# Latent attention with keys in partitions: maxima from a one-pass product, weights summed by additions

## The chip, the cores and the metric

The kernel runs on one core of one Trainium2 chip. The metric is the device time of one execution in microseconds (us). The engines are TensorE (PE, matrix products), VectorE (DVE), ScalarE (ACT), GpSimd (POOL) and SyncE (SP, which issues most of the transfers). The kernel keeps PE's results in eight PSUM banks of 128 partitions by 512 float32 columns, and everything else in SBUF.

## What is computed

The reference is a diffusion transformer of two layers on 256 context tokens and 1024 latent tokens of width 1024. Each layer has an input projection into three groups of heads (gated linear attention, retention, and eight heads of latent attention), an output projection, and a gated convolutional feed-forward part. The change concerns latent attention alone:

```python
def _mla_attend(qn, qr, kn, kr, v):
    s = (jnp.einsum('bqhd,bkhd->bhqk', qn, kn)
         + jnp.einsum('bqhr,bkr->bhqk', qr, kr)).astype(jnp.float32) * MLA_SCALE
    p = jax.nn.softmax(s, axis=-1).astype(v.dtype)
    return jnp.einsum('bhqk,bkhe->bqhe', p, v)
```

A query has 64 features without and 32 with rotation, 96 in all; a head's values have 64. Latent queries see all 1280 keys, context queries the 256 context keys. In the second layer no context output is needed. Everything is float32; a projection or score is computed as three products of the operands' high and low parts (hi by hi, lo by hi, hi by lo).

## The kernel before

A layer is a row of stages: the input projection (`proj`, whose matmuls are those of line 323), then linear attention (`lin`) and latent attention (`mla`) side by side, then the output projection (`wout`) and the feed-forward part. `lin` and `mla` are Python generators, and `weave` takes 1.1 steps of `lin` (`LIN_RATE`) for every step of `mla`. Each step emits some instructions; a scheduler then sets the final order of each engine, which the engine keeps to.

`mla` goes through the eight heads. `prod_v` makes the values of a pair of heads, `prod_qr` the rotated queries of four heads, and `prod_kq` keys and queries of one head, split into hi and lo, in tiles `h` of 96 used partitions (features) by 1280 tokens. What the next head needs is emitted beside the present one (`side`).

A unit is 128 queries of one head; a latent unit does this:

- `scores` (line 919): queries in partitions, keys along the columns, three products each for 512, 512 and 256 keys into three banks (`three` flips between banks 0 to 2 and 3 to 5). DVE takes the maximum of the first 1024 columns (921) and of the last 256 (924) and makes the negated, scaled maximum of both (928). ACT takes the exponentials in two pieces into the tile `w` (932), with their sums as a second output.
- `turn`: PE transposes the ten 128x128 blocks of weights (945) into the unit's own score banks; ACT (949, twice) and DVE (947) copy them to SBUF.
- `values`, once for two units: the value tile of 64 columns is stationary, the turned weights of 128 queries stream through it (969); the first unit writes the upper, the second the lower half of the partitions of bank `av`, in turn. DVE adds the two partial sums (962) and takes the reciprocal of 128x1 (963), POOL makes a diagonal matrix of it (965), PE spreads it by a product with ones (974), ACT copies that (976), and DVE multiplies (979) into a tile `y` for two heads.
- A transfer (983) writes `y` to DRAM (`S.m`) in two pieces per pair of heads; `wout` reads it back.

Layer 0 has two more units per head, the context's queries with 256 keys (`qp == 0`). The rotating buffers that matter are seven of `w2` (weights and turned weights) and five of `dgt`.

Of linear attention, DVE work with both operands in SBUF (lines 693, 703) and POOL products of 128x512 (716) recur below. The splits of weights and activations into hi and lo end in the subtraction of line 213.

Of the kernel before, what the change touches and what calls it, by code (L numbers as in the profile page):

```python
# [9 lines left out]
F32 = mybir.dt.float32  # L10
# [9 lines left out]
T = 1280  # L20
# [54 lines left out]
class Net:  # L75
# [53 lines left out]
    def dgt(self):  # L129
        return self.sb.tile([128, 128], F32, tag="dgt", bufs=5, name=self.nm("dg"))  # L130
# [34 lines left out]
    def wplan(self):  # L165
        """The split weights in the order of their use."""
# [57 lines left out]
    def explog(self, after=None):  # L224
        """The table set with both exp and ln, before a run of them."""
# [22 lines left out]
    def ada(self, l, sets, alloc=None):  # L248
        """Modulation, for both kinds of tokens, of 1024 features at a time: of a section, or of a half of sections 0 and 1."""
# [39 lines left out]
    def modulate(self, l, sec, c0, c1, src, F):  # L289
        """F[k] = src(k) * (1 + scale) + shift; src(k) may be F[k] itself."""  # L290
# [25 lines left out]
    def dense(self, ps, segs, wu, h, ks=range(8)):  # L316
        """ps[:, i, :n] = w.T @ h[:, o:o + n] over 8 K tiles, or the ks of them, for the i-th (o, n) of segs."""
# [8 lines left out]
    def rstd(self, ps, segs, scale, eps, al):  # L326
        """(sum * scale + eps) ** -0.5 in SBUF."""
# [30 lines left out]
    def begin(self, h, n):  # L358
        """The first half of K for the first n tiles of the projection: steps for their weights, then for a K tile of one."""
# [11 lines left out]
    def proj(self, l, b, h, S):  # L371
        """A step for every tile of the projection's columns."""
# [40 lines left out]
        def t3():  # L413
# [11 lines left out]
            # sums of log gates within chunks, [0] from the right and [1] from the left  # L425
# [115 lines left out]
    def lin_tables(self, l, S):  # L541
# [10 lines left out]
        # rows of iota: t + 1, 127 - t, 128 - t, t;  lg: 0..1 by partition (fwd, bwd), 2 + 4 * dir + head  # L552
# [18 lines left out]
    def lin_states(self, l, S):  # L571
        """The chunks' k^T v sums, and from them the state before every chunk, in both directions."""
# [4 lines left out]
        for g in range(5):  # L577
# [4 lines left out]
            for r in range(2):  # L582
# [27 lines left out]
                # the sums lie where the state after their chunk belongs  # L610
# [18 lines left out]
    def lin_chunk_out(self, S, r, c, qv, cs, v, rhs, oS):  # L629
        """o (pair, chunk) = states' part + rhs(h)'s part, into oS."""  # L630
# [44 lines left out]
    def gla_out(self, l, S, g):  # L675
# [11 lines left out]
        def factors(ns):  # L687
            """[0]: q's factor exp(sum from the middle of its block of 2n), [1]: k times its factor."""
# [19 lines left out]
        def expands(i, ns):  # L708
            """q of every head in rows of its own, times its factor."""
# [46 lines left out]
        # products of neighbours and of equal tokens: their sums over a head are columns  # L756
# [69 lines left out]
    def mla(self, l, S):  # L826
        nc, a = self.nc, self.a
# [9 lines left out]
        flip = [0]  # L837

        def three(keep=False):
            b = flip[0] ^ 3  # L840
            if not keep:
                flip[0] = b
            return self.ps[:, b:b + 3, :].rearrange("p a b -> p (a b)")

        def prod_v(p):
            V[p] = [self.hid([128, 5, 128]) for _ in range(2)]
            ps = three(keep=True)
# [7 lines left out]
        def prod_qr(x):  # L855
            QR[x] = [self.yk(F32R), self.yk(F32R)]
            ps, raw = three(keep=True), QR[x][1]
# [18 lines left out]
        def prod_kq(h):  # L876
# [14 lines left out]
            ps = three(keep=True)  # L891
# [15 lines left out]
        def scores(h, qp, i):  # L907
            """Weights of 128 queries, without their sums' division."""
            ctxq = qp == 0
            K, q = Kt[h % 2], Q[h]  # L910
            qs = slice(256 * qp + 128 * i, 256 * qp + 128 * i + 128)
            order = ((0, 0), (1, 0), (0, 1))
            st = self.sm([128, 8])
            sc = three()
            nk = CTX if ctxq else T
            for o in range(0, nk, 512):
                n = min(512, nk - o)
                for x, (qa, ka) in enumerate(order):
                    nc.tensor.matmul(sc[:, o:o + n], q[qa][0:96, qs], K[ka][0:96, o:o + n], start=(x == 0), stop=(x == 2))  # L919
                if o == 512:  # L920
                    nc.vector.tensor_reduce(st[:, 1:2], sc[:, 0:1024], axis=AX.X, op=ALU.max)  # L921
                if o + n < nk:
                    yield
            nc.vector.tensor_reduce(st[:, 0:1], sc[:, o:nk], axis=AX.X, op=ALU.max)
            if ctxq:
                nc.vector.tensor_scalar(st[:, 2:3], st[:, 0:1], -MSCALE, None, op0=ALU.mult)
            else:
                nc.vector.tensor_scalar(st[:, 2:3], st[:, 0:1], st[:, 1:2], -MSCALE, op0=ALU.max, op1=ALU.mult)  # L928
            P = self.w2([128, T], F32)
            # two pieces, for the first bank's transposes to start beside the second  # L930
            for j, (c0, c1) in enumerate([(0, nk)] if ctxq else [(0, 512), (512, nk)]):
                nc.scalar.activation(P[:, c0:c1], sc[:, c0:c1], AF.Exp, bias=st[:, 2:3], scale=MSCALE, accum_out=st[:, 3 + j:4 + j])  # L932
            ready.append(((h, qp, i), P, st, nk // 128, sc))
            yield

        ready, pts, vals, cur = [], [], [], []

        def turn(u):
            (h, qp, i), P, st, nk, sc = u
            pT = self.w2([128, 10, 128], F32)  # L940
            for gi, t0 in enumerate(range(0, nk, 4)):
                n = min(4, nk - t0)
                ps = sc[:, 128 * t0:128 * (t0 + n)].rearrange("p (a b) -> p a b", b=128)
                for t_ in range(n):
                    nc.tensor.transpose(ps[:, t_], P[:, 128 * (t0 + t_):128 * (t0 + t_) + 128], self.ident[:])  # L945
                if gi == 1:
                    nc.vector.tensor_copy(pT[:, t0:t0 + n], ps[:, 0:n])  # L947
                else:
                    nc.scalar.copy(pT[:, t0:t0 + n], ps[:, 0:n])  # L949
                if t0 + n < nk:  # L950
                    yield
            pts.append((pT, st))
            if i:
                vals.append(values(h, qp, [p for p, _ in pts], [t for _, t in pts], nk))
                pts.clear()

        def values(h, qp, pts, sts, nk):
            r = 64 * (h % 2)
            dgs = []
            for st in sts:  # L960
# [507 lines left out]
```

## Time and profile before

| | us |
|---|---|
| median of three runs | 3470.79 (3468.51 to 3471.84) |
| span of the profiled execution | 3473.9 |
| PE busy | 3383.5 (97%) |
| DVE busy | 2227.2 (64%) |
| ACT busy | 1548.3 (45%) |
| POOL busy | 398.5 (11%) |

The profiled execution's own time is that span, 3473.9 us; nothing of it lies around the span in what was recorded. Shares of the whole span are means over stages with different limits, so the table of stretches is to be read by stage. Matmuls are pipelined: the duration of one (some 0.29 to 0.64 us) is longer than the step from one start to the next, so the price of PE's work is read from the starts of a timeline. A float32 matmul that is not split into hi and lo has two records per instruction, a product of hi and lo parts and a transpose have one.

### The profile page before, as it was taken

The numbers are of one execution on the slowest core, as the hardware profiler recorded it, in microseconds if no ns is written. First come the engines' busy times: TensorE is split into PE (matmuls) and PEld (weight loads), VectorE is DVE, ScalarE is ACT, GpSimd is POOL, SyncE is SP. The second block draws the span as 40 slices with busy tenths as digits, with TensorE's granted clock in tenths as the row PEclk, the third lists the DMA queues.
The fourth block names the chain that finished last, engine by engine and source line by source line (L and its number), as shares of the span: only waits on it lengthen the run. The fifth ranks groups of instructions, "written<-read, shape, count | busy, mean of one in ns | idle before, by whom it ended". The sixth has DMA issues, their size and how long they took to land. (4 is left out here: it accounts for less than half of the span.)

```text
span 3473.9 us, 58101 instructions
## 1 busy us (share of the span) xinstructions
PE 3383.5 (97%) x23454; PEld 2919.4 (84%) x23454; DVE 2227.2 (64%) x3787; ACT 1548.3 (45%) x2867; POOL 398.5 (11%) x627
## 2 busy tenths in 40 slices
PE   8999999989999999999999999999999999999998
PEld 6997666768999999899999898766777888888897
DVE  3435878776774444675557734788877765687555
ACT  3334555544453333343334444555563544345433
POOL 0000333331010000000000000333310000001001
PEclk9999999989999999999999999999999999999999
DMA  8654111124223333432223444111124333323331
GB/s 291 203 185 135 29 55 41 40 83 141 74 73 116 122 116 132 147 104 78 75 73 120 161 135 136 36 42 51 38 96 131 96 92 97 97 91 116 98 92 49
DMA packets 174990, 354.95 MB, mean 102 GB/s; under 512 B 15552, under 2 KB 92160, under 8 KB 174720
## 3 DMA queue, kind: packets, MB, share of 16 engines
q1 hardware_dynamic: 174720, 351.23, 31.7%
q8 instruction: 184, 3.01, 0.4%
q14 instruction: 86, 0.70, 0.1%
HBM read 310.01 MB, written 36.44 MB: 100 GB/s over the span
## 5 line engine op out<-in xcount | busy, mean ns | idle before, releaser
L323 PE MATMUL ps<-h,w 128*128 128x320 f32 (+5 forms) x9600 | 1667.4, 334 | 15.1 <-ACT h L212 6.3
L323 PEld LDWEIGHTS ps<-h,w 128*128 128x128 f32 x9600 | 1532.0, 190 | 145.7 <-issue 7.0
L213 DVE TENSOR_TENSOR w<-ws,w 128x1024 fp32r<-128x1024 f32 x360 | 440.1, 1223 | 590.5 <-PE ps L323 294.5
L1180 PE MATMUL ps<-hid,w 128*128 128x256 f32 (+4 forms) x3696 | 576.6, 316 | 1.5 <-ACT hid L212 1.5
L1180 PEld LDWEIGHTS ps<-hid,w 128*128 128x128 f32 x3696 | 538.9, 189 | 36.1 <-issue 7.6
L212 ACT CAST w<-ws 128x1024 fp32r<-128x1024 f32 x360 | 378.8, 1053 | 416.6 <-PE ps L1180 291.2
L919 PE MATMUL ps<-h,h 96*128 96x512 f32 (+1 forms) x1200 | 325.4, 392 | 18.7 <-DVE w L947 14.4
L919 PEld LDWEIGHTS ps<-h,h 96*128 96x128 f32 x1200 | 200.0, 194 | 78.1 <-issue 21.1
L1147 DVE SCALAR_TENSOR_TENSOR t<-u,vec,t 128x642 f32<-128x642 f32 (+3 forms) x176 | 144.6, 821 | 181.9 <-ACT t L1146 181.8
L932 ACT ACTIVATE w<-ps,sm 128x768 f32<-128x768 f32 (+2 forms) x272 | 208.9, 774 | 113.0 <-DVE sm L928 91.2
L1141 ACT COPY u<-ps 128x512 f32<-128x512 f32 (+4 forms) x264 | 118.2, 483 | 310.7 <-PE ps L323 310.7
L1185 DVE SCALAR_TENSOR_TENSOR y<-ps,mod,y 128x320 f32<-128x320 f32 (+5 forms) x376 | 197.0, 557 | 69.0 <-PE ps L1180 68.3
L945 PE MATMUL ps<-ident,w 128*128 128x128 f32 x1312 | 222.3, 287 | 12.1 <-ACT w L932 12.0
L945 PEld LDWEIGHTS ps<-ident,w 128*128 128x128 f32 x1312 | 152.0, 144 | 70.6 <-issue 35.5
L965 POOL TENSOR_SCALAR dg<-ident,sm 128x128 f32<-128x128 f32 x144 | 99.8, 697 | 954.7 <-DVE sm L963 833.4
L1137 POOL MEMSET u<- 128x1 f32 (+1 forms) x264 | 20.9, 102 | 1616.9 <-DVE t L1148 1462.4
L969 PE MATMUL ps<-w,hid 128*64 128x128 f32 x2624 | 196.8, 282 | 3.8 <-DVE y L979 2.0
L969 PEld LDWEIGHTS ps<-w,hid 128*64 128x64 f32 x2624 | 151.8, 139 | 41.2 <-issue 29.1
L921 DVE TENSOR_REDUCE sm<-ps 128x1 f32<-128x1024 f32 x128 | 156.3, 1221 | 43.8 <-PE ps L919 38.8
L949 ACT COPY w<-ps 128x256 f32<-128x256 f32 (+1 forms) x272 | 128.2, 474 | 94.0 <-PE ps L945 92.0
L716 POOL TENSOR_TENSOR hid<-hid,hid 128x512 f32<-128x512 f32 x108 | 146.3, 1371 | 98.5 <-ACT hid L696 69.0
L1146 ACT ACTIVATE t<-u,vec 128x642 f32<-128x642 f32 (+3 forms) x176 | 153.8, 874 | 0.4
(195 smaller groups left out, 3279.4 us busy)
## 6 DMA issues: line engine op xcount, KB each, us to landing
ws<-in_up_dram SPq DMA_DIRECT2D x176, 512.0 KB, 3.6
ws<-in_down_dram SPq DMA_DIRECT2D x88, 512.0 KB, 3.5
ws<-in_ada_dram SPq DMA_DIRECT2D x80, 512.0 KB, 4.8
ws<-in_w_in_dram SPq DMA_DIRECT2D x48, 512.0 KB, 4.3
ws<-in_w_out_dram SPq DMA_DIRECT2D x32, 512.0 KB, 3.7
y<-in_ada_dram SPq DMA_DIRECT2D x16, 512.0 KB, 8.3
ws<-in_w_v_dram SPq DMA_DIRECT2D x16, 512.0 KB, 4.0
hid<-in_xT_dram SPq DMA_DIRECT2D x16, 320.0 KB, 6.1
```

What stands on the lines that cost most here:

```text
L212: self.nc.scalar.copy(hi, src)
L213: self.nc.vector.tensor_tensor(lo, src, hi.bitcast(F32), op=ALU.subtract)
L323: nc.tensor.matmul(ps[:, i, 0:n], w_[:, k, :], h[k][:, part, o:o + n], start=(k == 0 and q == 0), stop=(k == 7 and q == 2))
L716: nc.gpsimd.tensor_tensor(X[n][:], blk(E[n][:, 0, cs[i]]), qx[:], op=ALU.mult)
L919: nc.tensor.matmul(sc[:, o:o + n], q[qa][0:96, qs], K[ka][0:96, o:o + n], start=(x == 0), stop=(x == 2))
L921: nc.vector.tensor_reduce(st[:, 1:2], sc[:, 0:1024], axis=AX.X, op=ALU.max)
L932: nc.scalar.activation(P[:, c0:c1], sc[:, c0:c1], AF.Exp, bias=st[:, 2:3], scale=MSCALE, accum_out=st[:, 3 + j:4 + j])
L945: nc.tensor.transpose(ps[:, t_], P[:, 128 * (t0 + t_):128 * (t0 + t_) + 128], self.ident[:])
L969: nc.tensor.matmul(op[64 * i:64 * i + 64, 0], V[h // 2][t_ // 5][:, t_ % 5, r:r + 64], pts[i][:, t_], start=(t_ == 0), stop=(t_ == nk - 1) ...
L1146: nc.scalar.activation(v[:, 0:n], u[:, 1:1 + n], AF.Identity, scale=cw(j, 1), bias=self.vec[l][:, V_CB + j:V_CB + j + 1])
L1180: nc.tensor.matmul(pb[i][:, 0:n], w[w_][:, x, ms], p.hh[f0 + x][hp][:, o - 1:o - 1 + n], start=(x == 0 and q == 0), stop=(x == gn - 1 and ...
L1185: nc.vector.scalar_tensor_tensor(t, pb[i][:, o:o + n], self.md(l, 5, m, who), t, op0=ALU.mult, op1=ALU.add)
```

## The change

Scores are now computed with keys in partitions, so that the exponentials come out in the form that the values' product needs; there are no transposes of weights. The maximum of a query would then lie across partitions, so it is taken ahead:

- `maxima` (lines 925 to 935 of the changed kernel): a single product, hi by hi, of 128 queries by 512, 512 and 256 keys into banks 0 to 2, DVE's maximum of each (926), then of the three (928). A product with the identity (932) turns the 128x8 maxima (128x10 in layer 0), ACT copies them negated, and two transfers on SP take them to DRAM (934) and back into partition 96 of the queries' hi tile (935). The keys' hi tile holds 1.0 in that partition, so the hi by hi product over 97 partitions subtracts the maximum. `maxima` of head h + 1 is emitted beside head h, two steps of `side` for each half of a key tile.
- `products` (942): three products of 128 keys by 512 queries into banks 3 to 5; ACT takes exponentials of 512 columns into `held[kt]`, 128x1024 for the 1024 latent queries.
- `values` (948), two key tiles later: two 64-column, 512-wide products with the two halves of the queries into the two halves of bank `av`. POOL adds tiles 1 to 6 onto tile 0 (1037), DVE tiles 8 and 9 onto tile 7 (1035), then both sums (1043).
- `quotient`: ACT copies `av`, two products with ones (959) sum the partitions and spread the sum, DVE takes the reciprocal of 128x512 (960) and multiplies twice 64x512 (963); all 1024 columns are stored at once after odd heads (965).
- `LIN_RATE` is 1.5 and `dgt` has two buffers. `prod_v`, `prod_qr` and `prod_kq` keep their instructions, at lines 858 to 913.

The removed functions are those printed above; of the diff the added side is given.

```diff
-LIN_RATE = 1.1
+LIN_RATE = 1.5
...
-        return self.sb.tile([128, 128], F32, tag="dgt", bufs=5, name=self.nm("dg"))
+        return self.sb.tile([128, 128], F32R, tag="dgt", bufs=2, name=self.nm("dg"))
...
+        for K in Kt:
+            nc.gpsimd.memset(K[0][96:97, :].bitcast(F32), 1.0)
...
-        def scores(h, qp, i):
-        def turn(u):
-        def values(h, qp, pts, sts, nk):
+        def maxima(h):
+            k0, q0 = Kt[h % 2][0], Q[h][0]
+            mx, part = self.sm([128, 10]), self.sm([128, 8, 3])
+            for qi in range(lo // 128, 10):
+                nk = CTX if qi < 2 else T
+                for j, o in enumerate(range(0, nk, 512)):
+                    n = min(512, nk - o)
+                    t = bank("pre")[:, 0:n]
+                    nc.tensor.matmul(t, q0[0:96, 128 * qi:128 * qi + 128], k0[0:96, o:o + n], start=True, stop=True)
+                    nc.vector.tensor_reduce(mx[:, qi:qi + 1] if qi < 2 else part[:, qi - 2, j:j + 1], t, axis=AX.X, op=ALU.max)
                     yield
+            nc.vector.tensor_reduce(mx[:, 2:10], part[:], axis=AX.X, op=ALU.max)
+            yield
+            n = 10 - lo // 128
+            t, r = bank("pre"), self.dgt()
+            nc.tensor.matmul(t[0:n, 0:128], mx[:, 10 - n:10], self.ident[:], start=True, stop=True)
+            nc.scalar.activation(r[0:n, :], t[0:n, 0:128], AF.Copy, scale=-1.0)
+            nc.sync.dma_start(S.mx[h, 10 - n:10, :], r[0:n, :].bitcast(F32))
+            nc.sync.dma_start(q0[96:97, lo:T].bitcast(F32), S.mx[h:h + 1].rearrange("h a b -> h (a b)")[:, lo:T])
+            yield
+
+        def products(h, kt, c0, t):
+            n = t.shape[-1]
+            for x, (qa, ka, rows) in enumerate(((0, 0, 97), (1, 0, 96), (0, 1, 96))):
+                nc.tensor.matmul(t, Kt[h % 2][ka][0:rows, 128 * kt:128 * kt + 128], Q[h][qa][0:rows, c0:c0 + n], start=(x == 0), stop=(x == 2))
+
+        def values(h, kt, P, n, last):
+            r = 64 * (h % 2)
+            op = self.pb("av")
+            for i in range(2):
+                nc.tensor.matmul(op[64 * i:64 * i + 64, 0:n], V[h // 2][kt // 5][:, kt % 5, r:r + 64], P[:, i], start=(kt == 0), stop=last,
+                                 skip_group_check=True)
+
+        def quotient(h, c0, n, P):
+            r = 64 * (h % 2)
+            o, ov, rb = ob[h // 2], self.tt([128, n]), self.tt([128, n])
+            nc.scalar.copy(ov[:], self.pb("av")[:, 0:n])
+            yield
+            t = bank("pre")[:, 0:n]
+            for i in range(2):
+                nc.tensor.matmul(t[64 * i:64 * i + 64, :], self.ones[:, 0:64], P[:, i], start=True, stop=True, skip_group_check=True)
+            nc.vector.reciprocal(rb[:], t)
...
+            for kt in range(12):
+                if kt < 10:
+                    held[kt] = self.w2([128, 2, 512], F32)
                 for i in range(2):
+                    if kt < 10:
+                        t = bank("sc")
+                        products(h, kt, CTX + 512 * i, t)
+                        nc.scalar.activation(held[kt][:, i], t, AF.Exp, scale=MSCALE)
+                        beside()
+                    if i == 0:
+                        tail()
+                    elif kt >= 2:
+                        k = kt - 2
+                        P = held[k]
+                        values(h, k, P, 512, k == 9)
+                        if k in (8, 9):
+                            nc.vector.tensor_tensor(held[7][:], held[7][:], P[:], op=ALU.add)
+                        elif 0 < k < 7:
+                            nc.gpsimd.tensor_tensor(held[0][:], held[0][:], P[:], op=ALU.add)
...
+            nc.vector.tensor_tensor(held[0][:], held[0][:], held[7][:], op=ALU.add)
+            tails.append(quotient(h, CTX, 512, held[0]))
```

PE before, late in layer 1 (in a name such as `w_24960` the number tells buffers apart; `h` are hi and lo tiles, `w` weights, `hid` values): a unit's scores with the transposes of the unit before it in between, then values.

```order
L919 MATMUL ps<-h_20222,h_24406 128x512
L919 MATMUL ps<-h_20222,h_24407 128x512
L919 MATMUL ps<-h_20223,h_24406 128x512
L945 MATMUL ps<-ident,w_24960 128x128 x4
L919 MATMUL ps<-h_20222,h_24406 128x256
L919 MATMUL ps<-h_20222,h_24407 128x256
L919 MATMUL ps<-h_20223,h_24406 128x256
L945 MATMUL ps<-ident,w_24960 128x128 x4
L969 MATMUL ps<-w_24855,hid_23984 64x128
L969 MATMUL ps<-w_24903,hid_23984 64x128
L969 MATMUL ps<-w_24855,hid_23984 64x128
L969 MATMUL ps<-w_24903,hid_23984 64x128
```

PE now, late in layer 1, around two key tiles of values: products, maxima of the next head, values.

```order
L948 MATMUL ps<-w_21506,hid_21364 64x512 x2
L942 MATMUL ps<-h_21112,h_18576 128x512
L942 MATMUL ps<-h_21113,h_18576 128x512
L942 MATMUL ps<-h_21112,h_18577 128x512
L942 MATMUL ps<-h_21112,h_18576 128x512
L942 MATMUL ps<-h_21113,h_18576 128x512
L942 MATMUL ps<-h_21112,h_18577 128x512
L925 MATMUL ps<-h_18578,h_21470 128x256
L948 MATMUL ps<-w_21552,hid_21364 64x512
L925 MATMUL ps<-h_18578,h_21470 128x512
L925 MATMUL ps<-h_18578,h_21470 128x256
L948 MATMUL ps<-w_21552,hid_21364 64x512
```

The transposes are gone; the two matmuls of `w_21506` stand side by side (first row), while maxima products stand between the two of `w_21552`.

DVE before, in the same place: one unit's maxima, copy and sums after another's.

```order
L921 TENSOR_REDUCE sm_24895<-ps 128x1
L924 TENSOR_REDUCE sm_24895<-ps 128x1
L947 COPY w_24903<-ps 128x512
L928 TENSOR_SCALAR sm_24895<-sm_24895 128x1
L962 TENSOR_TENSOR sm_24847<-sm_24847 128x1
L963 RECIPROCAL sm_24847<-sm_24847 128x1
L962 TENSOR_TENSOR sm_24895<-sm_24895 128x1
L979 TENSOR_TENSOR y_24191<-ps,dg_24934 64x128 x2
```

DVE now, shortly ahead of PE's rows above: maxima (926), a quotient (960 and 963) and copies of linear attention (636, 743, 745).

```order
L926 TENSOR_REDUCE sm_21499<-ps 128x1
L743 COPY_PREDICATED hid_21532<-msk,ps 128x128
L636 TENSOR_TENSOR hid_21587<-y_18763,hm 128x512
L960 RECIPROCAL t_21462<-ps 128x512
L926 TENSOR_REDUCE sm_21499<-ps 128x1 x3
L963 TENSOR_TENSOR y_20755<-t_21461,t_21462 64x512 x2
L745 COPY_PREDICATED hid_21532<-msk,ps 128x128
L926 TENSOR_REDUCE sm_21499<-ps 128x1
L745 COPY_PREDICATED hid_21532<-msk,ps 128x128
L926 TENSOR_REDUCE sm_21499<-ps 128x1
```

In place of reductions of 1024 and 256 columns, a copy and small sums for each unit there are reductions of at most 512, one by one between linear attention's instructions, and a wide reciprocal per head.

## Rows read from the trace of the kernel before

**Rows 1.** The page: the span and its instructions

```profile
span 3473.9 us, 58101 instructions
```

**Rows 2.** Stretches: length, busy us (instructions) of PE, PEld, DVE, ACT, POOL, clock, DMA, GB/s

```profile
300.00:822.00 522.00, 491.60 (x4224) 355.63 (x4224) 404.45 (x879) 285.65 (x739) 172.67 (x180) 0.97 0.20 62
2134.00:2610.00 476.00, 458.46 (x4006) 337.25 (x4005) 374.43 (x773) 266.03 (x664) 140.02 (x146) 0.98 0.21 66
```

**Rows 3.** PE waits, 300 to 822 us: us in total, times, longest

```profile
PE ps L919 <- DVE w L947: 11.2, 8, 3.1
PE ps L945 <- ACT w L932: 10.7, 13, 2.1
```

**Rows 4.** PE waits, 2134 to 2610 us

```profile
PE ps L919 <- DVE w L947: 3.2, 5, 1.1
...
PE ps L945 <- ACT w L932: 1.3, 1, 1.3
```

**Rows 5.** Timeline of PE in layer 1: start, busy us, instruction, count

```profile
2572.99 1.31 PE L969 MATMUL ps<-w,hid 128*64 128x128 f32 x20
2574.23 0.44 PE L945 MATMUL ps<-ident,w 128*128 128x128 f32 x2
2574.42 1.64 PE L919 MATMUL ps<-h,h 96*128 96x512 f32 x6
2575.90 0.60 PE L945 MATMUL ps<-ident,w 128*128 128x128 f32 x4
2576.26 0.61 PE L919 MATMUL ps<-h,h 96*128 96x256 f32 x3
2576.70 0.60 PE L945 MATMUL ps<-ident,w 128*128 128x128 f32 x4
2577.24 1.31 PE L969 MATMUL ps<-w,hid 128*64 128x128 f32 x20
2578.38 0.39 PE L974 MATMUL ps<-dg,ones 128*64 128x128 f32 x4
```

**Rows 6.** Timeline of PE in layer 0: products of 64 columns, 512 wide

```profile
336.21 0.64 PE L897 MATMUL ps<-y,ws 128*64 128x512 f32 x1
336.22 0.64 PE L894 MATMUL ps<-y,ws 128*64 128x512 f32 x1
336.69 0.59 PE L897 MATMUL ps<-y,ws 128*64 128x512 f32 x1
...
337.12 1.45 PE L897 MATMUL ps<-y,ws 128*64 128x512 f32 x3
```

**Rows 7.** DVE lines, 300 to 822 us: count | busy us, mean ns | idle before

```profile
L921 DVE TENSOR_REDUCE sm<-ps 128x1 f32<-128x1024 f32 x64 | 78.1, 1221 | 20.3 <-PE ps L919 16.0 <-ACT hid L696 1.1 <-ACT hid L649 1.0
L947 DVE COPY w<-ps 128x512 f32<-128x512 f32 x64 | 43.7, 683 | 10.4 <-PE ps L945 10.1 <-ACT w L949 0.2
L924 DVE TENSOR_REDUCE sm<-ps 128x1 f32<-128x256 f32 x80 | 33.2, 416 | 8.3 <-PE ps L919 7.9
...
L979 DVE TENSOR_TENSOR y<-ps,dg 64x128 f32<-64x128 f32 x77 | 22.0, 286 | 3.4 <-ACT dg L976 2.2
...
L962 DVE TENSOR_TENSOR sm<-sm 128x1 f32<-128x1 f32 x64 | 16.2, 261 | 14.7 <-ACT w L932 14.3
...
L963 DVE RECIPROCAL sm<-sm 128x1 f32<-128x1 f32 x79 | 11.6, 158 | 3.4 <-ACT w L932 2.0
```

**Rows 8.** The page: a group of DVE, busy us, mean ns

```profile
L213 DVE TENSOR_TENSOR w<-ws,w 128x1024 fp32r<-128x1024 f32 x360 | 440.1, 1223 | 590.5 <-PE ps L323 294.5
```

**Rows 9.** By source line: count, ns min/median/max, first and last start

```profile
L441 DVE TENSOR_TENSOR_SCAN t<-ones,t x40: 394/399/880, 83.9 to 2078.1; 128x128 f32<-128x128 f32 x40
...
L716 POOL TENSOR_TENSOR hid<-hid,hid x108: 1262/1286/1773, 348.4 to 2505.4; 128x512 f32<-128x512 f32 x108
...
L703 DVE TENSOR_TENSOR hid<-hid,u x54: 403/598/1495, 355.5 to 2498.2; 128x256 f32<-128x256 f32 x54
```

**Rows 10.** The page: transfers of a tile, KB each, us to landing

```profile
h<-y SPq DMA_DIRECT2D x64, 64.0 KB, 2.0
```

More of the change, by code (lines that the diff above doesn't have):

```diff
@@ L856, in prod_qr @@
             QR[x] = [self.yk(F32R), self.yk(F32R)]
-            ps, raw = three(keep=True), QR[x][1]
+            ps, raw = three(), QR[x][1]
             chunks = [(o, min(512, T - o), ps[:, o - lo:min(512 + o, T) - lo]) for o in range(lo, T, 512)]
@@ L890, in prod_kq @@
             yield
-            ps = three(keep=True)
+            ps = three()
             for o, t, kb in ((CTX, ps[:, 0:512], 1), (CTX + 512, ps[:, 512:1024], 1), (0, ps[:, 1024:1280], 0)):
@@ L936, in mla @@
-        ready, pts, vals, cur = [], [], [], []
-        def turn(u):
[L939 to L955, printed above, removed]
@@ L987, in chain, with tail @@
                 yield from g
+        tails = []
+        def tail():
+            if tails and next(tails[0], self) is self:
+                tails.pop(0)
         for _ in chain(prod_v(0), prod_qr(0), prod_kq(0)):
             yield
-        side = None
-        def step(n=1):
-            while cur and n:
-                n -= 1
-                if next(cur[0], self) is self:
-                    cur.pop()
-        def start():
-            cur.append(turn(ready.pop(0)))
-            step()
-        def value():
-            if vals and next(vals[0], self) is self:
-                vals.pop(0)
+        base[0] = 0
+        for i, _ in enumerate(maxima(0)):
+            if i % 2:
+                yield
         for h in range(8):
-            if side is not None:
-                for _ in side:
-                    pass
             if h % 2 == 0:
@@ L1017, in mla @@
                     g.append(prod_qr((h + 1) // 4))
-                g.append(prod_kq(h + 1))
+                g += [prod_kq(h + 1), maxima(h + 1)]
                 if (h + 1) % 2 == 0:
@@ L1021, in mla @@
             side = chain(*g)
-            for qp in range(l, 5):
-                for i in range(2):
-                    for j, _ in enumerate(scores(h, qp, i)):
-                        if qp and j == 0:
-                            yield
-                            continue
-                        if (qp == 0 or j == 1) and ready:
-                            start()
-                        if qp == 0 or j == 2:
-                            step()
-                            if qp:
-                                yield
-                            value()
-                            step()
-                        yield
-                    if qp > l:
-                        next(side, None)
@@ L1039, in mla, with beside @@
-        start()
-        step(4)
-        while vals:
-            value()
+            def beside(n=2):
+                for _ in range(n):
+                    next(side, None)
+            if l == 0:
+                P = [self.w2([128, 2, 128], F32) for _ in range(2)]
+                for kt in range(2):
+                    t = bank("sc")[:, 0:256]
+                    products(h, kt, 0, t)
+                    nc.scalar.activation(P[kt][:].rearrange("p a b -> p (a b)"), t, AF.Exp, scale=MSCALE)
+                beside()
+                tail()
+                yield
+                tail()
+                tail()
+                for kt in range(2):
+                    values(h, kt, P[kt], 128, kt == 1)
+                nc.vector.tensor_tensor(P[0][:], P[0][:], P[1][:], op=ALU.add)
+                tails.append(quotient(h, 0, 128, P[0]))
+                tail()
+                del P
+                yield
@@ L1045, in wout @@
+            nc.vector.tensor_tensor(held[0][:], held[0][:], held[7][:], op=ALU.add)
+            tails.append(quotient(h, CTX, 512, held[0]))
+            tail()
+            for _ in side:
+                pass
+            del held
+        while tails:
+            tail()
     def wout(self, l, c0, c1, h, y):
```

73 lines of the change are left out of this document (20 added, 53 removed).

## Prediction

> **What bounds the kernel now.** I read first the table of stretches [rows 2]: latent attention runs in 300 to 822 us (layer 0) and 2134 to 2610 us (layer 1), 998 us of the profiled execution's 3473.9 [rows 1]. The other 2476 us hold no instruction that the change edits, so I count them at no change. In both stretches TensorE (PE) is the bound: 491.60 of 522 us (94%) and 458.46 of 476 (96%), at a granted clock of 0.97 and 0.98, the 2.4 GHz level. VectorE (DVE) comes second with 404.45 (77%) and 374.43 us (79%), ScalarE (ACT) has about 55%, GpSimd (POOL) 33% and 29%. So the change is worth what it does to PE's own work in these 998 us, plus what it does to PE's idle time, 30.4 and 17.5 us. What ends that idle time stands in the waits [rows 3, 4]: the score banks, which the copies of line 947 free, and the exponentials of line 932, ahead of the transposes. The four rows sum to 26.4 us.
>
> PE's price for a unit (128 queries of one head) comes from a stretch late in layer 1 in which it does not wait [rows 5]. From start to start: values 1.24 us (20 records: 10 instructions, two records each), transposes 0.19 + 0.36 + 0.54 = 1.09, scores 1.48 for six of 512 columns (0.247 each) and 0.44 for three of 256 (0.147); 4.25 in all. The ones product adds about 0.39 per two units.
>
> **PE's work per head of 1024 queries.** Removed: transposes, 8 x 1.09 = 8.7 us. The rest was values 8 x 1.24 = 9.9, scores 8 x 1.92 = 15.4, ones 4 x 0.39 = 1.6; 35.6 with the transposes. Now: products, 10 key tiles x 2 halves x 3 = 60 of 512 columns, 60 x 0.247 = 14.8. Maxima, for each 128 queries 0.247 x 2 + 0.147: 8 x 0.64 = 5.1. Values: 10 pairs of 64-column, 512-wide matmuls. The nearest rows are the key and query products of the same shape [rows 6]: two that write different halves of the columns start 0.01 us apart, and the next two 0.48 us later; three by themselves take 1.45 us, of which 337.12 less 336.69 = 0.43 is one step. A pair of instructions (two records each) is thus 0.91 us if its halves run together and 2 x 0.86 = 1.72 if not. All pairs together: 9.1, and 0.9 for the ones pair. Sum 14.8 + 5.1 + 9.1 + 0.9 = 29.9, or 5.7 less per head, **46 us less per layer**. (A context unit of layer 0 changes by under 0.3 us per head; left out.)
>
> That sum needs the two halves to stand next to each other on PE. In the built order many don't: a maxima product or a product of linear attention, meant to fill in, lands between them (in PE's excerpt the pair of `w_21552`, while that of `w_21506` is whole). Of the 160 pairs of values at 512 columns, 53 of 80 are split in layer 0 and 37 of 80 in layer 1; some split by another 64-column matmul keep a partner, so I count 45 and 37 that stand alone. Each loses 0.81 us. A change of width costs too: four transposes ahead of scores take 0.36 us, four ahead of values 0.54 [rows 5], so 0.18 for each further entry into half columns. 82 x 0.99 = 81 us given back of 2 x 46 = 92. Entries that aren't splits rise from 8 to about 11 per head, 16 x 3 x 0.18 = 9. Together **-2 us**: PE's work does not change. This is the step on which the forecast rests, and its price is read from a neighbour's shape: between nothing lost (a split pair still overlapping) and all of it, I take all, since a matmul of full width lies between the halves and needs both.
>
> **The other engines.** DVE in layer 0 loses the score reductions, copies, sums, small reciprocals and products, 78.1 + 43.7 + 33.2 + 22.0 + 16.2 + 11.6 = 205 us [rows 7]. It gains 16 reductions of 512 and 10 of 256 per head (0.68 by the copy of 512 and 0.416: 15.0), three adds of 128x1024 (1.22 each [rows 8]: 3.7), a reciprocal of 128x512, two 64x512 products (1.4), and 1.3 for context: 22.1 per head with the reciprocal at 0.7, 177 per layer. The reciprocal is bounded by 0.68 (one pass, like the copy) and by 4 x 0.399 = 1.6 (the scan of 128 columns, the dearest row per column [rows 9]); I take 0.7, as the 128x1 form (158 ns, against 261 for an addition of the same size [rows 7]) shows no dearness. POOL gains 48 adds of 128x1024 per layer. Twice L716's 1286 ns at 512 [rows 9] is 2.6 us each, 123 us; with its 172.67 [rows 2] that is at most 57% of layer 0's stretch, and it hides under PE. But L703, a DVE addition with both operands in SBUF, takes 403 to 1495 ns [rows 9]: at worst 1.1 us more, nearly an L716. So a POOL add can hold such a DVE operation by 0 to 2.6 us. I take 0.8 an add, 38 us per layer. DVE then stands at 404 - 205 + 177 + 38 = 414, about where it was: it neither frees nor bounds the stage on the mean. The Trainium skill ("SBUF — State Buffer", section "Who interferes with whom") speaks against this part: it calls the port pair that DVE shares with GpSimd an exclusive lock. L703's spread agrees; held for the whole length at every add, it gives rival 3. ACT loses its copies and accumulates and stays hidden.
>
> **The waits.** Removed: the 26 us of [rows 3, 4], whose producers are gone. New, each with its bounds:
> - Head 0's maxima have no head to run beside. Their 26 reductions take 15 us on DVE while PE has 5 us of maxima and what linear attention it is given (1.5 steps for each step of attention); then the negated maxima go to DRAM and back, two transfers at the 2.0 us of h<-y [rows 10], before the first product, on SyncE's queue, behind linear attention's stores. 0 to 15 us, taken 6 per layer: 12.
> - At the end everything of the last head is divided and stored at once: two adds 2.4, the ones pair 0.9, reciprocal 0.7, two products 1.4, against small sums, one diagonal and two products of 0.29 before. 3 to 5 us later in layer 0; in layer 1 output-projection matmuls stand between. Sum 5.
> - 14 turns of heads: keys, queries, maxima, DRAM and back must end before the next head's first product; prod_kq and prod_v cover some of it. 0 to 5 us, taken 1: 14.
> - PE now queues 24 or 26 single maxima products per head, whose three banks wait for DVE. When linear attention's burst stands ahead on DVE, PE's in-order queue waits with products and values behind it. Three banks cover 3 x 0.68 = 2 us. 0 to 25 us, taken 11 in all.
>
> New 42, old 26: +16. **Sum**: -2 + 16 = +14 us on the profile's own 3473.9; the runs' median lies 3 us below that, 3470.8 + 14 = **3485 us**. What one measurement of this kernel can tell from no change is about 0.2%, 7 us, so 3464 to 3478 counts as no change.
>
> **Rivals.**
> 1. Split pairs cost little. If a matmul on the left half runs on beside what comes next, the 81 us come back in part: 3485 - 81 = 3404 at the whole, 3440 at half. For: the shape that prices it [rows 6] was only seen alone or paired. Against: PE's rows in [rows 5] run one after the other at each change of width. Chance 0.2.
> 2. The decoupling works: exponentials no longer wait for a maximum, so turns and DVE bursts (14 + 11) cost nothing and more than the named 26 us of idle time goes: 3485 - 25 - 10 = 3450. For: POOL and ACT have room. Against: DVE is as full as before. Chance 0.15.
> 3. DVE becomes the bound (slower). POOL's adds hold it for 2.6 us each: 123 us per layer in place of 38 puts it at 414 + 85 = 499 of 522 us, 96%, and PE waits at the maxima banks. It decides once DVE's share passes PE's, some 92%. The part beyond, 20 us per layer, is lost and the waits double (+ 11): 3485 + 40 + 11 = 3536. Against: most of DVE's new work reads PSUM. Chance 0.1.
> 4. A dear reciprocal. If it works each column eight times, its slope (0.683 - 0.416 for 256 columns [rows 7], 0.53 for 512) gives 8 x 0.53 = 4.3 us in place of 0.7. Two last heads pay 3.6 each in full, 14 turns what three banks don't cover, 1.6: 7 + 22 = 29, 3514. The Trainium skill ("VectorE: DVE Perf Modes", section "First, the fixed hardware budget") names a repeat count of 8 for this operation; no row here shows more than one column of it. Chance 0.15.
>
> **How the numbers follow.** The forecast has 0.4: its own range, from the waits' bounds, is 3462 to 3510. Faster: rivals 1 and 2, 0.35, and a little of the forecast, 0.37. Same: the forecast's lower third, 0.13. Slower: the rest of it and rivals 3 and 4, 0.50. Eight in ten lie between 3427 (half and more of rival 1 kept) and 3536 (most of rival 3 kept).
>
> **What would show it.** In the trace of after: L948 records with a maxima product between them should stand 0.8 us longer than adjacent ones, and PE's busy time in the two stretches should be within 15 us of 950. If it is 60 or more lower, rival 1 holds. L960's mean decides rival 4 (0.7 or 4.3 us). L703 and the adds of L1035 grown to 2 us and more, with DVE over 90%, show rival 3. PE's waits should name L926 at the maxima banks, and gaps ahead of the first L942 of each head should be 6 us at head 0 and 1 at the others. What would make it wrong: PE's idle time in the stages above 90 us, or below 30.

## Result and the profile after

The changed kernel takes 3636.88 us (median of four runs, 3629.72 to 3642.12) against 3471.32: a ratio of 1.0474 (95% interval 1.0459 to 1.0489). That is **slower, as forecast, but by 166 us instead of 14**, and outside the range. The profiled execution's span went from 3473.9 [rows 1] to 3635.2 us.

The page of the kernel after, its span, engines and the two DVE and POOL groups that are new:

```profile
span 3635.2 us, 50748 instructions
PE 3471.4 (95%) x20270; PEld 2749.7 (76%) x20270; DVE 2331.7 (64%) x3371; ACT 1410.1 (39%) x2355; POOL 561.8 (15%) x583
...
L926 DVE TENSOR_REDUCE sm<-ps 128x1 f32<-128x512 f32 (+1 forms) x400 | 221.7, 585 | 92.2 <-PE ps L925 90.3
L1037 POOL TENSOR_TENSOR w<-w,w 128x1024 f32<-128x1024 f32 x96 | 238.7, 2487 | 271.1 <-PE ps L948 173.0
```

The two stages, cut from the last projection matmul to the first output-projection matmul: first the kernel before, then the kernel after. Columns as in [rows 2]: length, busy us of PE, PEld, DVE, ACT, POOL, granted clock, DMA.

```profile
308.40:821.40 513.00, 482.61 (x4110) 347.31 (x4109) 399.56 (x869) 281.00 (x726) 172.57 (x180) 0.97 0.19 60
2158.60:2605.10 446.50, 430.00 (x3735) 313.76 (x3733) 355.69 (x742) 251.06 (x626) 140.02 (x146) 0.98 0.18 56
```

```profile
310.10:905.10 595.00, 530.27 (x2555) 263.30 (x2553) 459.10 (x653) 207.78 (x453) 248.31 (x149) 0.90 0.16 49
2248.50:2753.40 504.90, 460.98 (x2192) 226.34 (x2190) 391.56 (x538) 182.28 (x383) 224.46 (x130) 0.93 0.15 45
```

The stages grew by 82 and 58 us, 140 of the span's 161; 21 lie outside, 13 of them after the last stage. DVE's share did not rise (78% and 80% before, 77% and 78% now). The granted clock fell, from 0.97 and 0.98 to 0.90 and 0.93.

To part PE's time I took each of its records in the stages from its start to its modelled end less 0.166 us (a 512-column record lasts 0.397 us, the next starts after 0.232), and joined them. Time in a stretch whose granted clock is 0.5 (1.2 GHz) counts half as work and half as loss; what no record covers is idle, small gaps between matmuls included. For all kernels but e10, both stages summed, in us. The parts are those of the profiled execution, the time is the median of all runs; the two differ by up to 8 us, in e12 by 14 (its profiled execution took 3563).

| kernel | time | stages | PE work at 2.4 GHz | lost at 1.2 GHz | PE idle |
|---|---|---|---|---|---|
| before | 3471 | 959.5 | 804 | 22 | 133 |
| after | 3637 | 1099.9 | 822 | 74 | 204 |
| e1 whole pairs | 3612 | 1074.5 | 747 | 110 | 218 |
| e2 reciprocal on ACT | 3606 | 1071.9 | 815 | 65 | 192 |
| e3 no POOL adds | 3542 | 1006.8 | 822 | 34 | 152 |
| e4 no maxima | 3560 | 1026.8 | 691 | 97 | 240 |
| e5 adds on DVE | 3588 | 1055.5 | 821 | 55 | 180 |
| e6 = e1 + e3 | 3467 | 934.0 | 747 | 37 | 150 |
| e7 = e1 + e2 + e5 | 3487 | 955.9 | 747 | 50 | 159 |
| e8 = e1 + e2, adds halved | 3565 | 1026.2 | 741 | 71 | 214 |
| e9 = e7, four tiles on PE | 3476 | 961.4 | 784 | 38 | 140 |
| e12 = before + 96 POOL adds | 3549 | 1046.9 | 806 | 47 | 194 |
| e13 = e1 + e2 + e3 | 3443 | 913.0 | 740 | 31 | 142 |

So after against before is +17 work, +52 clock, +71 idle, and the 21 outside: the span's 161. (In the expectations below idle time stands some us lower, 200 for after and 145 for e6, and the gains of e1 and e3 as 26 and 95 us.)

Of the idle time, the waits that the profile names (0.15 us and longer) grew from 45 to 108 us in the two stages. Two groups make up most of it: waits ahead of linear attention's matmuls (lines 600 to 810) rose from 10 to 47 us, and 41 us end with a reduction of the maxima, of which these two rows are the longest (layer 0, layer 1: us in total, times, longest):

```profile
PE ps L925 <- DVE sm L926: 14.2, 13, 4.2
PE ps L925 <- DVE sm L926: 11.1, 9, 2.2
```

The idle time has a face in the trace. DVE, POOL and PE of the kernel after near 845 us (start, busy us, instruction, count, [idle before and its releaser]):

```profile
843.88 0.94 DVE L960 RECIPROCAL t<-ps 128x128 f32<-128x128 f32 x1
844.75 0.22 DVE L741 COPY hid<-ps 128x128 f32<-128x128 f32 x1
845.00 4.58 DVE L963 TENSOR_TENSOR y<-t,t 64x128 f32<-64x128 f32 x2
849.62 0.64 DVE L743 COPY_PREDICATED hid<-msk,ps 128x128 f32<-128x128 uint8 x2
850.29 0.30 DVE L745 COPY_PREDICATED hid<-msk,ps 128x128 f32<-128x128 uint8 x1
850.49 1.92 DVE L636 TENSOR_TENSOR hid<-y,hm 128x512 f32<-128x512 f32 x1
```

```profile
844.64 7.22 POOL L1037 TENSOR_TENSOR w<-w,w 128x1024 f32<-128x1024 f32 x3 [1.93 <-PE ps L948]
```

```profile
846.00 1.07 PE L948 MATMUL ps<-w,hid 128*64 128x512 f32 x2
852.67 1.23 PE L643 MATMUL ps<-hid,hid 128*128 128x128 f32 x4 [5.60 <-DVE hid L745]
```

Two products of 64x128, 0.27 us at the shortest, take 4.58 us while POOL adds: each goes on when a POOL addition ends. The copies that linear attention's next matmul needs stand behind them, and PE is idle for 5.6 us. In the whole trace 63 DVE instructions that last over 0.3 us longer than the shortest of their form overlap an L1037, and 59 of them would, with their shortest duration, have started within 0.15 us of a POOL add's end; the other four, of another POOL instruction's end (L716, L806). Where its operands lie decides whether an instruction is held: every form among the 63 reads two operands from SBUF, while 153 instructions that read one from PSUM beside an add (926, 913, 960 and others) last at most 0.07 us longer than the shortest of their form. A product with both operands in SBUF, and the maxima, by source line (count, ns min/median/max):

```profile
L963 DVE TENSOR_TENSOR y<-t,t x48: 274/690/2831, 376.5 to 2764.4; 64x512 f32<-64x512 f32 x32, 64x128 f32<-64x128 f32 x16
L926 DVE TENSOR_REDUCE sm<-ps x400: 362/677/694, 323.2 to 2709.1; 128x1 f32<-128x256 f32 x94, 128x1 f32<-128x512 f32 x40
```

DVE counts as busy while it is held, so its share shows nothing of this.

### The profile page after: what moved, and what is told of

The parts are those of the page before. It is cut to its first block, busy times and chain, and to the rows that moved or that the text cites. A ratio compares the mean times of both kernels' runs of the same rounds, so it can differ in the third digit from the quotient of the medians.

```text
span 3635.2 us, 50748 instructions
## 1 busy us (share of the span) xinstructions
PE 3471.4 (95%) x20270; PEld 2749.7 (76%) x20270; DVE 2331.7 (64%) x3371; ACT 1410.1 (39%) x2355; POOL 561.8 (15%) x583
## 5 line engine op out<-in xcount | busy, mean ns | idle before, releaser
L1026 ACT ACTIVATE w<-ps 128x512 f32<-128x512 f32 x320 | 188.7, 596 | 338.5 <-PE ps L942 332.4
L942 PE MATMUL ps<-h,h 96*128 96x512 f32 (+3 forms) x1008 | 318.7, 431 | 0.3 <-ACT w L1026 0.2
L942 PEld LDWEIGHTS ps<-h,h 96*128 96x128 f32 (+1 forms) x1008 | 183.3, 199 | 151.8 <-issue 92.2
L926 DVE TENSOR_REDUCE sm<-ps 128x1 f32<-128x512 f32 (+1 forms) x400 | 221.7, 585 | 92.2 <-PE ps L925 90.3
L1037 POOL TENSOR_TENSOR w<-w,w 128x1024 f32<-128x1024 f32 x96 | 238.7, 2487 | 271.1 <-PE ps L948 173.0
L948 PE MATMUL ps<-w,hid 128*64 128x512 f32 (+1 forms) x704 | 276.0, 614 | 0.3 <-ACT w L1005 0.3
L1155 DVE SCALAR_TENSOR_TENSOR t<-u,vec,t 128x642 f32<-128x642 f32 (+3 forms) x176 | 144.6, 822 | 183.8 <-ACT t L1154 183.6
L925 PE MATMUL ps<-h,h 96*128 96x512 f32 (+1 forms) x400 | 156.1, 440 | 34.5 <-DVE sm L926 25.3
L925 PEld LDWEIGHTS ps<-h,h 96*128 96x128 f32 x400 | 77.8, 206 | 126.5 <-DVE sm L926 66.6
L716 POOL TENSOR_TENSOR hid<-hid,hid 128x512 f32<-128x512 f32 x108 | 153.3, 1439 | 83.0 <-ACT hid L696 56.2
L1156 DVE SCALAR_TENSOR_TENSOR t<-u,vec,t 128x642 f32<-128x642 f32 (+3 forms) x176 | 144.3, 820 | 11.4
L212 ACT CAST hid<-t 128x642 fp32r<-128x642 f32 (+3 forms) x88 | 59.5, 676 | 204.8 <-DVE t L1160 204.8
```

Of the source, the lines that this page charges most:

```text
L212: self.nc.scalar.copy(hi, src)
L925: nc.tensor.matmul(t, q0[0:96, 128 * qi:128 * qi + 128], k0[0:96, o:o + n], start=True, stop=True)
L926: nc.vector.tensor_reduce(mx[:, qi:qi + 1] if qi < 2 else part[:, qi - 2, j:j + 1], t, axis=AX.X, op=ALU.max)
L942: nc.tensor.matmul(t, Kt[h % 2][ka][0:rows, 128 * kt:128 * kt + 128], Q[h][qa][0:rows, c0:c0 + n], start=(x == 0), stop=(x == 2))
L948: nc.tensor.matmul(op[64 * i:64 * i + 64, 0:n], V[h // 2][kt // 5][:, kt % 5, r:r + 64], P[:, i], start=(kt == 0), stop=last, skip_group_c ...
L1026: nc.scalar.activation(held[kt][:, i], t, AF.Exp, scale=MSCALE)
```

## Experiments

Three theories. **A**: DVE is late, held by POOL's additions and by a dear reciprocal; PE waits, and the clock falls with the waits. **B**: the split pairs of values cost the time. **C**: the clock falls with the new shapes, whatever the waits.

**e1, whole pairs.** The second matmul of a pair gets priority and is pinned behind the first; no pair is split.

```diff
+                with self.tc.high_priority() if i else ExitStack():
+                    m = nc.tensor.matmul(op[64 * i:64 * i + 64, 0:n], ...)
+                    if i:
+                        self.tc.keep_in_program_order(m)
```

> The changed kernel, with the two 64-column matmuls of every pair of values kept next to each other on PE (all 160 pairs whole, where 90 are split in the changed kernel). Theory B (the split pairs are what costs): PE's work at full clock falls by 82 x 0.8 = 66 us, idle time and clock stay as they are, time 3571 us or less. Theory A (DVE is late: POOL's adds hold its SBUF operations and a reciprocal takes 3.35 us; PE waits, and the clock falls with the waits): PE reaches the same waits earlier, most of the gain becomes idle time, 3600 to 3625 us. Theory C (the clock falls because of the new shapes and not because of waits): PE time at the half clock stays near 148 us in the two stages, about 3571 us.

Measured 3611.51 us, ratio to before 1.0395 (1.0365 to 1.0425): 25 us less. PE's work fell by 75 us, as B says, but 36 more are lost at 1.2 GHz and 14 more are idle. The time lies in A's range: PE finishes sooner and waits for the same late work. But A had idle time take most of the gain, and it is the clock that takes the larger part.

**e2, reciprocal on ACT.**

```diff
-            nc.vector.reciprocal(rb[:], t)
+            nc.scalar.activation(rb[:], t, AF.Ln)
+            nc.scalar.activation(rb[:], rb[:], AF.Exp, scale=-1.0)
```

> The changed kernel, with the reciprocal of the sums taken on ACT as exp(-ln(x)), two passes of about 0.6 us there, in place of 3.35 us on DVE. Theory A: 16 x 3.35 + 8 x 0.95 = 61 us leave DVE; PE's waits fall by about half of it and the half-clock time with them, 3590 to 3615 us. Theory B: within 10 us of the changed kernel's 3637.

Measured 3606.3 us, ratio 1.0387 (1.0366 to 1.0408): 31 us less, as A expected; in the stages idle time falls by 12, the clock's loss by 9 and PE's work by 7. The row it removes, from the kernel after by source line (count, ns min/median/max):

```profile
L960 DVE RECIPROCAL t<-ps x24: 940/3350/3359, 370.8 to 2759.8; 128x512 f32<-128x512 f32 x16, 128x128 f32<-128x128 f32 x8
```

**e3, no additions on POOL.**

```diff
-                        elif 0 < k < 7:
-                            nc.gpsimd.tensor_tensor(held[0][:], held[0][:], P[:], op=ALU.add)
```

> The changed kernel without POOL's 96 additions of 128x1024 (the sums leave out key tiles 1 to 6, and the exponentials are scaled by 0.001 so that the partial sums stay finite; all other work as before). Theory A: the holds of DVE go (its excess over the shortest of each form falls from 213 us in the two stages to about 80), PE's idle time falls from 200 to about 140 us and the half-clock loss from 74 to 40: 3530 to 3575 us. Theory B: PE's work unchanged, 3625 to 3640 us. Theory C: idle falls and the half-clock time doesn't: about 3590 us.

Measured 3542.4 us, ratio 1.0205 (1.0188 to 1.0222): 94 us less, with PE's work unchanged at 822. Idle falls by 52 and the clock's loss by 41 us. DVE's excess (the durations of its instructions in the stages less the shortest of each form) falls from 221 to 113 us (89 in the kernel before). The largest single share, on A's side; its stages:

```profile
309.20:845.40 536.20, 501.62 (x2555) 252.87 (x2554) 401.28 (x653) 207.20 (x453) 124.77 (x101) 0.95 0.18 55
2189.70:2660.30 470.60, 445.50 (x2191) 223.65 (x2189) 343.00 (x538) 182.37 (x383) 103.25 (x82) 0.95 0.17 52
```

**e4, no maxima.** `maxima` only sets partition 96 of the queries to zero.

> The changed kernel without the maxima: no one-pass product, no reductions, no round trip through DRAM; partition 96 of the queries is set to zero, and the exponentials are scaled by 0.001 so that they stay finite. 89 us of PE's work and 230 us of DVE's go. Theory A: PE waits for DVE no more at the maxima banks, idle time falls below 110 us and half-clock loss below 30: 3410 to 3460 us, under the kernel before. Theory B: the pairs split by maxima products (48 of 160 split now, not 90) give 35 us, the maxima 89: about 3510 us. Theory C: half-clock time stays: about 3545 us or 3510 with the pairs.

Measured 3560.36 us, ratio 1.0262 (1.024 to 1.0285): a miss by 100 us for A as I had put it. C's 3545 is nearest, but the loss at 1.2 GHz, which it had unchanged, rose by 22 us. PE's work fell by 131 us and DVE's by 126, and yet idle time rose by 35. The waits for maxima are gone, but others stand in their place: 134 of 158 us of named waits are now ahead of linear attention's matmuls. The longest in layer 0 of this run (total, times, longest):

```profile
PE ps L727 <- POOL hid L716: 14.7, 11, 5.7
PE ps L739 <- POOL hid L716: 14.1, 2, 10.1
PE ps L643 <- DVE hid L636: 11.0, 5, 3.6
PE ps L647 <- DVE t L750: 10.3, 4, 5.3
```

All four wait for linear attention's own products: L716 stands in POOL's queue among the adds, L636 and L750 are held on DVE. The wait of 10.1 us ends at 619 us; before it POOL makes six adds in a row, and DVE is held, three products of 0.67 us at the shortest taking 8.33 us (start, busy us):

```profile
600.22 16.20 POOL L1021 TENSOR_TENSOR w<-w,w 128x1024 f32<-128x1024 f32 x6 [2.25 <-PE ps L932]
608.65 8.33 DVE L693 TENSOR_TENSOR hid<-u 128x512 f32<-128x512 f32 x3
```

So removing what PE waits for at one place uncovers the next late chain. The run is not a clean removal, though: setting the partition to zero puts 16 instructions of about 1 us into POOL's queue, and POOL stands idle for 88 us ahead of them, with linear attention's products right behind in 8 cases. What that added was not parted from the rest.

**e5, the adds on DVE** (`gpsimd` becomes `vector` in that line).

> The changed kernel, with the 96 additions of 128x1024 on DVE (1.22 us each, 117 us more of its work) in place of POOL. If POOL's adds cost through the hold on DVE's SBUF operations and through POOL's queue (linear attention's products stand behind them), both go, against 117 us more work on DVE: 3570 to 3610 us. If they cost as a mere load, DVE, the fuller engine, makes it worse: 3650 us or more.

Measured 3588.16 us, ratio 1.0325 (1.0307 to 1.0342). 117 us more work on the fuller engine is 49 us faster than the same work on POOL: the adds cost by what they hold up.

**e6, whole pairs without the adds.**

> Pairs of values whole and POOL's additions left out (sums lack key tiles 1 to 6, exponentials scaled by 0.001). By themselves the two gave 26 and 95 us. If the 75 us of PE work that whole pairs save were eaten by waits that POOL's adds cause, the two together give more than their sum, 3637 - 95 - 60 = 3480 us or less. If the clock falls with the share of time in which PE works, whatever the waits come from, the pairs give again only some 25 us: about 3515 us, with the half-clock loss back above 60 us.

Measured 3466.66 us, ratio 0.9983 (0.9974 to 0.9993). By themselves 25 and 94, together 170 us. The 75 us of PE work arrive in full once nothing holds DVE and POOL, and the clock's loss is 37, not above 60.

**e7, whole pairs, reciprocal on ACT, adds on DVE**, an exact kernel.

> Whole pairs, the reciprocal on ACT, the additions on DVE. Theory A (late DVE and POOL, clock as a consequence): DVE loses 61 us of reciprocals and the holds and gains 117 us of adds; PE's work is 75 us less: 3490 to 3540 us, not under the kernel before's 3473 since DVE now stands near 90% of the stages. Theory C (the new shapes alone let the clock fall): half-clock loss as in the whole pairs' run, above 100 us, 3560 us or more.

Measured 3487.23 us, ratio 1.0038 (1.0023 to 1.0053), 3 us below A's range. In the stages it is 4 us shorter than before; the rest lies outside.

**e8, as e7 with the adds on POOL in halves of 512 columns.**

> Whole pairs, the reciprocal on ACT, POOL's additions cut into halves of 128x512 (192 in all, 1.2 us each). If a hold lasts as long as one POOL instruction, the longest DVE stalls halve while their sum stays near: 3560 to 3590 us, some 10 to 20 us under what pairs and reciprocal give without it (about 3580). If the length of one POOL instruction doesn't matter, 3580 or more (more instructions on POOL).

Measured 3564.56 us, ratio 1.0258 (1.0241 to 1.0274). Within what was expected of shorter holds, but pairs and reciprocal alone were not run, so it does not tell by how much they help; 77 us over e7 show that halved adds on POOL still cost.

**e9, four tiles summed by the ones product.**

```diff
-            tails.append(quotient(h, CTX, 512, held[0]))
+            tails.append(quotient(h, CTX, 512, [held[k] for k in (0, 7, 8, 9)]))
...
+            for j, p in enumerate(P):
+                    m = nc.tensor.matmul(..., p[:, i], start=(j == 0), stop=(j == len(P) - 1), ...)
...
+                if h % 2:
+                    nc.sync.dma_start(S.m[:, 4 + h // 2, c], o[:, c])
```

> Whole pairs, reciprocal on ACT, and of the additions only tiles 1 to 6, on DVE; the product with ones sums tiles 0, 7, 8 and 9 in its bank (three more pairs per head on PE, 22 us per layer; three additions fewer on DVE, 29 us per layer, and none of them between the last values and the quotient), and each half of the queries is stored by itself. Against the run with whole pairs, reciprocal on ACT and all additions on DVE (3487 us): if DVE, 94% busy there in layer 0, bounds the stage, 20 to 35 us less, 3450 to 3470 us, under the kernel before; if PE's work bounds it, 20 to 40 us more.

Measured 3476.07 us, ratio 1.0012 (1.0003 to 1.0021): 11 us under e7, half of the least that was expected, and not under the kernel before. The gain is outside the stages: they are 6 us longer than e7's, but what lies outside fell from 15 to 3 us over the kernel before. The run changes two things there, the last additions and the storing by halves, and does not part them.

**e10, LIN_RATE 1.7 on e9.**

> As the run with four tiles summed by the product with ones, with LIN_RATE 1.7 in place of 1.5. Linear attention is what ends last in both stages of the run before it (PE idle 6.6 us ahead of the output projection in layer 0): if that tail costs, 5 to 10 us less than that run; if the mixture on DVE is what counts, no change or up to 10 us more.

Measured 3481.09 us, ratio 1.0022 (1.0013 to 1.0031): 5 us more than e9, nothing gained. In the kernel after itself neither LIN_RATE nor the two buffers of `dgt` was varied.

**e12, the kernel before with 96 POOL adds.** Each doubles in place a tile of weights that nothing reads again.

```diff
+            if qp > 1:
+                nc.gpsimd.tensor_tensor(P[:, 0:1024], P[:, 0:1024], P[:, 0:1024], op=ALU.add)
             pts.append((pT, st))
```

> The kernel before, unchanged but for 96 more POOL additions of 128x1024 (48 per layer), each on a tile of weights that its transposes have read and that nothing reads again. No new shape on PE, PE's order all but the same. Theory A (POOL's long additions hold DVE's SBUF operations and linear attention's POOL work, PE waits, and the clock falls with the waits): 50 to 100 us over the kernel before, PE idle time up by 30 us or more and the half-clock loss from 22 to above 35 us. Theory C (the clock falls with the new shapes): half-clock loss stays near 22 us. If only the new order is sensitive to late DVE work: under 15 us.

Measured 3549.39 us, ratio 1.023 (1.021 to 1.0249): 76 us for additions that no engine waits for, and shorter ones than the kernel after has (1.89 us each, against 2.39). In the profiled execution, 14 us over the median, PE's work is the same within 2 us, idle rises by 61, the clock's loss by 25 and DVE's excess by 73 us (89 to 163), without any new shape. The additions, then its stages:

```profile
L953 POOL TENSOR_TENSOR w<-w x96: 1885/1894/2447, 354.7 to 2692.3; 128x1024 f32<-128x1024 f32 x96
310.80:879.40 568.60, 505.31 (x4112) 358.14 (x4110) 439.81 (x868) 282.42 (x722) 275.22 (x228) 0.94 0.17 54
2214.60:2692.90 478.30, 442.01 (x3735) 318.03 (x3733) 386.22 (x742) 251.68 (x627) 239.24 (x194) 0.96 0.17 54
```

**e13, all three out.**

> All three suspects out at once: whole pairs, reciprocal on ACT, POOL's additions left out (sums lack key tiles 1 to 6, exponentials scaled by 0.001). Whole pairs without the additions took 3467 us; the reciprocal gave 31 us beside late DVE work. Theory A: with DVE relieved of another 61 us the idle time falls from 145 to about 125 us and the half-clock loss from 37 to about 25: 3435 to 3450 us. If a part of the half-clock time belongs to the new shapes, idle falls but the half-clock loss stays near 37: 3450 to 3460 us. If what is left waits for linear attention's own chain, no change from 3467.

Measured 3443.08 us, ratio 0.9918 (0.9905 to 0.9932): 194 us under the kernel after and 28 under the kernel before. Idle time and the clock's loss fell to 142 and 31 us, less far than A had put them. This is what the arrangement would give if the sums of tiles 1 to 6 were free. They aren't, and no exact version that I ran beats the kernel before.

## Why the prediction was right or wrong

- **The sign.** Slower was right, in part by luck. Of the 161 us, 52 are the clock, which the sum had at nothing, and 52 of the 71 us of idle time go with POOL's additions (e3), which it had found harmless.
- **The bound and PE's work.** The bound of the kernel before was read rightly, and PE's work moved by +17 us against a sum of -2. The split pairs were priced at 81 us and cost 75 (e1); in layer 0 the values' row reads 138.2 us split and 94.1 whole (kernel after, then e1; clock included):

```profile
L948 PE MATMUL ps<-w,hid 128*64 128x512 f32 x320 | 138.2, 647 | 0.0
```

```profile
L949 PE MATMUL ps<-w,hid 128*64 128x512 f32 x320 | 94.1, 677 | 0.0
```

  With whole pairs the arrangement saves 58 us of PE's work, not the 83 (92 less 9) that I had: the mis-sized term there, and no run tells which of its prices was too low. Rival 1 is out: a pair with a full-width matmul between its halves does lose its overlap.
- **The waits, the step that failed first.** I put +16 us on new waits and measured +71; by PE's busy time, which the prediction went by, idle rose from 47 to 109 us, past the 90 that were to show it wrong. The step was "0.8 us an add" for POOL's holds, booked as load on DVE and found harmless because DVE's share stayed the same. The size was near (the 63 held instructions lose 101 us over 96 adds, 1.1 us each), and the share did stay the same. But a hold delays a single instruction by up to 2.3 us in a chain DVE, POOL, PE that linear attention runs through, and the adds also stand in POOL's queue ahead of linear attention's products (17 of these start straight behind one). Together that costs 94 us (e3) and, in the kernel before, 76 (e12); no run parts the holds from the queue. The sum had no term for waits ahead of linear attention's matmuls, which grew by 37 us, and gave the maxima banks 11 us (0 to 25), where 41 were measured; without the adds (e3) these two groups are at 21 and 23 us. The Trainium skill's exclusive lock ("SBUF — State Buffer", section "Who interferes with whom") agrees with 59 of 63 held instructions that go on when a POOL add ends.
- **The clock, missing from the sum.** 52 us. PE's idle time in the stages and the loss at 1.2 GHz rise together (133 and 22 before, 194 and 47 in e12, 204 and 74 after, 218 and 110 in e1). The first such stretch of layer 0 in the kernel after begins at 334.6 us, amid head 0's maxima, after 26 us in which PE is idle for 5.0 in pieces (first row); at 1.2 GHz PE then waits for the same reductions again:

```profile
308.00:334.00 26.00, 21.01 (x230) 11.61 (x228) 20.16 (x38) 10.16 (x35) 0.00 (x0) 1.00 0.55 163
334.00:347.00 13.00, 9.28 (x112) 6.05 (x112) 11.65 (x27) 4.99 (x20) 3.04 (x3) 0.52 0.19 54
347.00:358.00 11.00, 6.50 (x14) 1.95 (x15) 10.93 (x21) 1.08 (x4) 6.48 (x5) 0.50 0.01 2
```

- **Rival 3** named the mechanism (POOL's adds hold DVE) and the direction, but had it decide only when DVE's share passes 92%, and gave it 51 us. DVE stood at 77%; e3 and e12 measure 94 and 76 us. It was given 0.1.
- **Rival 4** was right in kind: 3.35 us where I took 0.7, and 31 us in e2 where it gave 29. That the two agree is in part luck, since 16 of the 31 are the clock and PE's work, which it did not have. By the Trainium skill's repeat count ("VectorE: DVE Perf Modes", section "First, the fixed hardware budget") my estimate was 4.3 us; the measured 3.35 decides. I had treated rivals 3 and 4 as exclusive; both came, on top of the sum.
- **Rival 2** is out: it had idle time fall, and it rose by 71 us.
- **The end.** "Sum 5" for storing the last head at once: 13 us were lost after the last stage, and the trace names most of them: the last columns are stored at once at 2765.1 us, PE waits 6.3 us for them to be read back, and from that wait on the granted clock is at 1.2 GHz for 10 us. In e9, with the last additions gone and each half stored by itself, 2 are left.

## What to carry to other kernels

An engine's busy share does not show whether it is late: an instruction that is held counts as busy, so look at the spread of durations within one form and at what the engine next to it was doing. Work moved to GpSimd is not free because GpSimd is idle; ask which VectorE instructions read two SBUF operands beside it and who waits for those. Where two column halves share TensorE, pin the pair; and count idle TensorE time as dearer than itself: in e12, 61 us more of it came with 25 us more lost at 1.2 GHz.

## What the runs showed of the hardware

- A DVE reciprocal takes 3.35 us for 128x512 and 0.94 us for 128x128, so 6.3 ns for each further column, against 1.0 ns for a copy ([rows 7]: 683 less 416 ns for 256 columns, across a copy and a reduction).
- A POOL addition of 128x1024 in float32 takes 2.39 us (median), and DVE instructions with two SBUF operands stretch to its end; those that read PSUM did not: L926 stays at 681 ns for 512 columns, L913 at 1.22 us.
- At nearly equal idle time the new arrangement loses more to the clock: 38 us in e9 against 22 before, at 140 and 133 us idle; 74 after against 47 in e12, at 204 and 194. Some 10 to 25 us thus go with the new matmuls or with where the idle time lies; no run separates the two, and this stays open.
